# Decoder step on one core: the heads' inverse on 32x32 blocks, one sample part, unbroken scores, w_out in two halves of the tokens

## The chip, the core and the metric

The kernel runs on one core of a Trainium2 chip. The metric is the device time of one execution in microseconds (us). Five engines work side by side, each through its own list of instructions in a fixed order: TensorE (PE, matrix products into PSUM), VectorE (DVE), ScalarE (ACT), GpSimd (POOL) and SyncE (SP, which issues most of the DMA transfers).

## What is computed

The reference is one layer of a decoder trunk in fp32. 512 tokens of a prompt and 8 requests of 4 sample tokens share the weights; the kernel works on all 544 at once.

```python
def trunk_layer(x, wkv0, shift0, conv0, p):
    x = layer_norm(ALPHA * x + 0.5 * swiglu(x, ffn1), ln1)
    proj = x @ p["w_in"]
    # RWKV-7 heads: r, k, v, decay w, a, gate g from the token-shifted part of proj; per token
    #   sa = S (-kk);  S = S * w + sa (kk * a)^T + v k^T;  o = S r
    y_rwkv = group_norm(o) + sum(r * k * r_k) * v, times g
    # short conv: u = c_c * c_h; z = cw[0] u[t] + cw[1] u[t+1] + cw[2] u[t+2]
    y_conv = c_b * z
    mix = concat([y_rwkv, y_conv]) @ p["w_out"]
    x = layer_norm(ALPHA * x + mix, ln2)
    return layer_norm(ALPHA * x + 0.5 * swiglu(x, ffn2), ln3), states
```

There are 8 heads of size 64, a model width of 1024 and an FFN width of 2816. The outputs are the tokens and the new states of the heads, the shift and the convolution.

## The kernel before

**Large products.** Weights and activations are split into a high and a low fp32r part (`split`, `wsplit`: ACT writes the high part, DVE the low part, L146 and L147 for weights), and a 128x128 weight block is applied in three products (`mm3`). The trace calls their PSUM tiles `mm` (3 buffers) and the other ones `sm` (5 buffers). A weight tile of 1024 columns comes through a ring of raw buffers and a ring of split buffers `hl`; `ex_hl` lengthens the second ring for a while.

**Stages.** FFN1 and its norm; projections; the heads and the convolution (the mixer); w_out with the second norm; FFN2 and the last norm. FFN1 and FFN2 lie outside the change. Tokens go in two halves, of 256 and of 288 (`HALF`).

**The heads.** Four pairs of heads, eight chunks of 64 prompt tokens and a ninth one for the 32 sample tokens. For each pair `scores` makes the triangular products of its chunks (into `SC`), stores the strict triangle A to DRAM (`Ad`), and transposes k and v into `BK` and `UV`; `off` then masks A to what lies off its 16x16 diagonal blocks. `elim` inverts the 64 unit triangular 64x64 matrices: the 16x16 diagonal blocks are gathered from DRAM, one to a partition and half (`AT`), and inverted on DVE in 15 steps of two instructions (L982, L984; result `De`); `De` and its transpose are written into zero-filled 64x64 frames in DRAM (`Dd`, filled at L823 to L829 from a part of UV that POOL clears), read back as `DM` and `XT`, and four rounds of 64 products with 64, 48, 32 and 16 columns finish the inverse in `XT`. Each round's results leave PSUM through ACT or DVE; after the first, POOL copies UV into SC (L1020). `sample` treats the ninth chunk, in two parts of two pairs: inverse of 4x4 blocks (`X8`), products with the loaded state (`S0`), W, UV, outputs, and for each head pair a masked copy `ux` (L1165) and a 512-wide product that updates the state. `chain` then goes through the eight chunks in order, three dependent groups of small products a chunk (W, UV, S).

**What sets the order.** The program is written out as generators. Critical ones (`scores`, `elim`, norms) yield a price; `weave` spends that price, times a factor of `FILL`, on the background list `bg` of large products (the projections of the convolution, then w_out). `take(n)` spends an absolute amount. In `elim` the background is an alternation (`alt`) of `sample` and the convolution. A scheduler may move instructions of an engine among independent ones; while `pinned` is set, PE keeps the written order.

**w_out.** After the chain the four tiles of the convolution rows (`wo_c`) run for both halves, woven with the norm of the heads (`gnorm`, four calls); then the four tiles of the head rows (`wo_r`), kept in the ring of 3+4, run for half 0 alone and for half 1 behind the second norm of half 0 (`l2a`). That is 96 large products behind the norm. The split of FFN2's first weights follows on ACT.

## Time and profile before

| | |
|---|---|
| median of 3 runs | 1123.34 us (1118.27 to 1123.51) |
| profiled execution | 1127.86 us, of which span 1126.1 us |
| granted TensorE clock, mean | 0.986 |
| PE busy | 1093.6 us (97%) |
| DVE, ACT, POOL busy | 833.2, 573.5, 198.5 us |
| chain that ended last | PE 89%; DMA, DVE and ACT 3% each |
| first scores of the last pair, first product of `sample` | 535.8 us, 549.0 us |
| start of the chain, end of the chain | 626 us, 662 us |
| end of w_out, first product of FFN2 | 728 us, 733 us |

The span runs from the first to the last instruction of the profiled execution; its own time is 1.8 us longer. Busy time is the sum over an engine's instructions without overlaps. A row of the timeline has start, duration, engine, line of the program, operation, `out<-in`, shape and count. An fp32 product of the small kind is two instructions in the trace, so 64 products stand as x128.

### The profile page before, as it was taken

To read this page: it belongs to the slowest core of one execution; us is meant where nothing else is said; L and a number is where in the kernel's file an instruction comes from. 1 tells how busy PE (TensorE), PEld (TensorE's weight loads), DVE (VectorE), ACT (ScalarE), POOL (GpSimd) and SP (SyncE) were. 2 spreads that over 40 slices of the span, in tenths; PEclk is the share of its full clock that TensorE was granted. 3 is DMA by queue.
4 is the path that set the end of the run, shared out by engine and by line. 5 is a ranking of instruction groups with operands and counts; after the bars stand their busy time and mean duration, and the time that the engine had idled before them with its cause. 6 is when DMAs were issued, how large, how long until landed. Compare 5 with 4: busy or idle time off the path is not lost.

```text
span 1126.1 us, 23085 instructions
## 1 busy us (share of the span) xinstructions
PE 1093.6 (97%) x9432; PEld 1047.8 (93%) x9432; DVE 833.2 (74%) x1521; ACT 573.5 (51%) x1056; POOL 198.5 (18%) x319
## 2 busy tenths in 40 slices
PE   9999999999999999999998899899999999999996
PEld 8999999999999988999887689899999999999995
DVE  7788988888776857667653556778979888896655
ACT  6645556555552574554213554367455565554524
POOL 0131221303100133132101420001312213131000
PEclk9999999999999999999998899989999999999999
DMA  8576685958751372312473511143676949586402
GB/s 291 114 155 166 141 199 126 216 130 185 165 161 41 117 153 67 86 49 70 113 103 115 178 60 57 41 150 76 136 185 131 208 111 220 141 171 145 118 1 80
DMA packets 100523, 145.64 MB, mean 129 GB/s; under 512 B 38976, under 2 KB 62912, under 8 KB 100416
## 3 DMA queue, kind: packets, MB, share of 16 engines
q1 hardware_dynamic: 73216, 107.97, 31.8%
q0 software_dynamic: 27200, 36.18, 20.9%
q8 instruction: 74, 1.21, 0.4%
q14 instruction: 33, 0.27, 0.1%
HBM read 124.70 MB, written 10.52 MB: 120 GB/s over the span
## 4 chain that ended last, share of the span: by engine, by line
PE 89%; DMA 3%; DVE 3%; ACT 3%; issue 1%; SPq 1%; POOL 0%; ACTq 0%; DVEq 0%
PE mm L75 55%; PE sm L75 34%; DMA z<-sv 1%; DMA DM<-Dd 1%; ACT hl L146 1%; DMA raw<-in_wd 1%; DVE hl L147 0%; DMA z<-in_xT 0%; SPq L697 0%; DMA yc<-ycd 0%; DMA BK<-in_w 0%; DVE z L261 0%; ACT z L252 0%; ACT L135 0%; DVE xhl L269 0%
## 5 line engine op out<-in xcount | busy, mean ns | idle before, releaser
L75 PE MATMUL mm<-xhl,hl 128*128 128x256 f32 (+2 forms) x2640 | 372.7, 296 | 5.8 <-ACT hl L146 5.0
L75 PEld LDWEIGHTS mm<-xhl,hl 128*128 128x128 f32 x2640 | 347.0, 191 | 20.8 <-issue 7.1
L147 DVE TENSOR_TENSOR hl<-raw,hl 128x1024 fp32r<-128x1024 f32 (+3 forms) x224 | 260.7, 1169 | 65.7 <-ACT hl L146 64.9
L146 ACT ACTIVATE hl<-raw 128x1024 fp32r<-128x1024 f32 (+3 forms) x224 | 224.2, 1012 | 80.0 <-DVE raw L486 31.1
L75 PE MATMUL sm<-xhl,hl 128*128 128x272 f32 (+1 forms) x1392 | 193.7, 289 | 0.4 <-DVE xhl L151 0.3
L75 PEld LDWEIGHTS sm<-xhl,hl 128*128 128x128 f32 x1392 | 182.0, 189 | 1.6 <-DVE xhl L151 0.8
L75 PE MATMUL mm<-tv,hl 128*128 128x272 f32 x864 | 122.0, 290 | 2.4 <-ACT cpb L586 2.4
L75 PE MATMUL mm<-hhl,hl 128*128 128x272 f32 (+2 forms) x792 | 119.2, 294 | 0.1
L75 PEld LDWEIGHTS mm<-tv,hl 128*128 128x128 f32 x864 | 114.0, 189 | 3.0 <-ACT cpb L586 2.6
L75 PEld LDWEIGHTS mm<-hhl,hl 128*128 128x128 f32 x792 | 105.9, 188 | 5.1 <-ACT sv L625 1.5
L75 PE MATMUL sm<-hhl,hl 128*128 128x272 f32 (+2 forms) x792 | 109.5, 288 | 0.0
L75 PEld LDWEIGHTS sm<-hhl,hl 128*128 128x128 f32 x792 | 102.9, 188 | 0.5
L492 POOL DMA_DIRECT2D raw<-in_gu x36 | 43.5, 1209 | 259.0 <-DVE cpb L582 84.3
L498 POOL DMA_DIRECT2D raw<-in_wd x32 | 39.3, 1470 | 279.2 <-DVE hlb L151 245.7
L75 PE MATMUL mm<-tv,hlb 128*128 128x272 f32 x432 | 61.1, 291 | 0.9 <-ACT cpb L589 0.9
L75 PEld LDWEIGHTS mm<-tv,hlb 128*128 128x128 f32 x432 | 56.4, 188 | 2.5 <-ACT cpb L589 2.4
L217 ACT ACTIVATE lnq<-z 128x512 f32<-128x512 f32 (+1 forms) x24 | 15.0, 654 | 53.7 <-DVE z L216 53.7
L150 ACT ACTIVATE hhl<-sv 128x272 fp32r<-128x272 f32 (+1 forms) x52 | 26.0, 512 | 30.5 <-DVE sv L349 12.1
L151 DVE TENSOR_TENSOR hlb<-raw,hlb 128x512 fp32r<-128x512 f32 x52 | 35.7, 686 | 5.5 <-ACT hlb L150 5.5
L150 ACT ACTIVATE hhl<-hk 128x272 fp32r<-128x272 f32 (+1 forms) x48 | 24.2, 504 | 27.5 <-DVE hk L556 12.9
L486 DVE TENSOR_TENSOR raw<-raw 128x512 f32<-128x512 f32 x52 | 35.8, 688 | 1.0
L75 PE MATMUL mm<-hhl,hlb 128*128 128x272 f32 (+2 forms) x264 | 36.4, 288 | 0.0
(300 smaller groups left out, 1391.7 us busy)
## 6 DMA issues: line engine op xcount, KB each, us to landing
raw<-in_gu SPq DMA_DIRECT2D x84, 512.0 KB, 4.7
raw<-in_gu POOLq DMA_DIRECT2D x36, 512.0 KB, 6.5
raw<-in_wd SPq DMA_DIRECT2D x32, 512.0 KB, 4.8
raw<-in_win SPq DMA_DIRECT2D x26, 512.0 KB, 3.5
raw<-in_wd POOLq DMA_DIRECT2D x32, 256.0 KB, 6.4
raw<-in_wd SPq DMA_DIRECT2D x16, 384.0 KB, 3.1
z<-cpb POOLq DMA_DIRECT2D x16, 272.0 KB, 8.8
z<-sv POOLq DMA_DIRECT2D x16, 272.0 KB, 7.5
```

What stands on the lines that cost most here:

```text
L75: ins = f(*args, **kw)
L146: ACT.activation(hl[:, 0, a:b], raw[:, a:b], AF.Copy)
L147: DVE.tensor_tensor(hl[:, 1, a:b], raw[:, a:b], hl[:, 0, a:b].bitcast(F32), op=OP.subtract)
L150: ACT.activation(hi, x, AF.Copy)
L151: DVE.tensor_tensor(lo, x, hi.bitcast(F32), op=OP.subtract)
L217: sq = ACT.activation(qq, zz, AF.Square)
L486: DVE.tensor_tensor(y[:, :, 0], y[:, :, 1], a[:, :, 1], op=OP.add)
L492: POOL.dma_start(x.rearrange("p (s c) -> p s c", s=2), bass.AP(tensor=a11.tensor, offset=a11.offset, ap=[[2 * D, P], [P * 2 * D, 2], [1, 5 ...
L498: POOL.dma_start(four(x)[:, i], bass.AP(tensor=a11.tensor, offset=a11.offset, ap=[[DFF, P], [P * DFF, 2], [1, 256]]), accum_op=OP.add)
```

## The change

1. **Inverse.** Blocks of 32x32, 31 steps of two instructions on up to 256 elements per partition (L964, L966 of the changed program); the results go to DRAM as whole rows of 4 KB, come back in pieces of 128 B, only the diagonal blocks, with no zero-filled frame; two rounds of 64 products 32x32 take the place of four. `off`, its mask and the zero fill are gone; POOL clears XT.
2. **Sample.** One part for all four pairs. The state comes in one transfer of 1 MB. One of the two `ux` of a pair and the last scaling of the state move from DVE to POOL.
3. **Scores.** The stops inside a pair go but for one of 600; PE is pinned there; the fills ahead of pairs become 2500 in place of 2000.
4. **w_out.** All eight weight tiles stay (ring 3+5). Order: convolution rows of half 0 beside the head norm of half 0, head rows of half 0 beside the norm of half 1, then all rows of half 1 behind the second norm, 192 products. PE is unpinned after the chain.

```diff
-FILL = dict(..., p0=2000, s=0.4, p3=2000, e0=1.0, e1=1.0, g=1.5, l2a=1.0, ...)
+FILL = dict(..., p0=2500, s=600, p3=2500, e0=1.0, e1=1.0, g0=1.0, g1=1.0, l2a=1.5, ...)
...
-    POOL.memset(uvf[:, 0:2048], 0.0)
...
-    for d in Dd:
-        for par in range(2):
-            dma(d[par, :, 0:64].rearrange("c s t -> s c t"), uvf[R(par), 0:2048].rearrange("p (c t) -> p c t", t=64))
+    Dd = [dr.tile([2, 32, 2, 32, 32], F32, name=f"Dd{i}") for i in range(2)]
...
-                yield 400
...
-            if p < 3:
-                self.off()
...
-        for g in range(2):
-            dma(AT[:, g], diag(Ad, g))
+        dma(AT, bass.AP(tensor=Ad.tensor, offset=Ad.offset, ap=[[2080, P], [64, 32], [1, 32]]))
...
+        for k in range(31):
+            n = 31 - k
+            tv = tm[:, :n * (k + 1)].rearrange("p (i j) -> p i j", j=k + 1)
+            DVE.tensor_tensor(tv, AT[:, k, k + 1:32, None].to_broadcast([P, n, k + 1]),
+                              De[:, k, None, 0:k + 1].to_broadcast([P, n, k + 1]), op=OP.mult)
+            DVE.tensor_tensor(De[:, k + 1:32, 0:k + 1], De[:, k + 1:32, 0:k + 1], tv, op=OP.add)
+            yield 550
+        DVE.tensor_copy(AT, De.rearrange("p a b -> p b a"))
         for d, x in zip(Dd, (De, AT)):
+            dma(d.rearrange("a c b s t -> (a c b) s t"), x)
+        B = lambda par, b: slice(64 * par + 32 * b, 64 * par + 32 * b + 32)
+        for i, (x, b) in enumerate(((DM, 0), (XT, 1), (XT, 0))):
             for par in range(2):
+                dma(x[B(par, b)].rearrange("p c d t -> p (c d) t")[:, :, 32 * b:32 * b + 32],
+                    Dd[i > 0][par, :, b].rearrange("c s t -> s c t"))
...
-        for rnd in range(4):
+        for rnd in range(2):
+            for c0 in range(0, 8, 4):
                 q = sm()
+                for c in range(c0, c0 + 4):
                     for pl, par in PLP:
+                        o = ((c - c0) * 4 + pl) * 32
+                        a, b = B(par, rnd), B(par, 1 - rnd)
+                        if rnd:
+                            lhs, rhs = DM[a, c, pl, :], XT[a, c, pl, 32:64]
+                        else:
+                            lhs, rhs = SC[a, pl, par, c, 32:64], DM[a, c, pl, :]
+                        PE.matmul(q[b, o:o + 32], lhs, rhs, start=True, stop=True)
...
-    def sample(g, cp):
+    def sample(cp):
...
+                (POOL if par else DVE).tensor_tensor(ux[par], UV[:, pl, par, 8, None, :].to_broadcast([P, NSEQ, 64]),
+                                  bmask[:, :, None].to_broadcast([P, NSEQ, 64]), op=OP.mult)
...
+            POOL.tensor_tensor(s0v, s0v, Pes[:, pl, :, None].to_broadcast([P, NSEQ, 64]), op=OP.mult)
...
-        weave("s", pairs[p].scores())
+        pinned[0] = True
+        for _ in pairs[p].scores():
+            take(FILL["s"])
+        pinned[0] = False
...
-    wstate["ex_hl"] = [lambda: w4.tile([P, 2, 1024], F32R, name="hl", bufs=4)] * 4
+    wstate["ex_hl"] = [lambda: w4.tile([P, 2, 1024], F32R, name="hl", bufs=5)] * 5
...
+    wc = [wload(wo_c[i]) for i in range(4)]
+    wr = [wload(wo_r[i]) for i in range(4)]
+    bg.append(wout(wc, KC, 0))
+    weave("g0", seq(gnorm(0, 0, yp), gnorm(1, 0, yp)))
     drain()
+    bg.append(wout(wr, KR, 0, True))
+    weave("g1", seq(gnorm(0, 1, yp), gnorm(1, 1, yp)))
+    drain()
+    bg.append(seq(wout(wc, KC, 1), wout(wr, KR, 1, True)))
     weave("l2a", layer_norm(z, 0, V_LN2G, V_LN2B, epsl, lnq, lnr, f2.s1[0], to_x(z, False)))
```

Three places in the order of instructions. The first is PE at the rounds of the inverse, before: `DM,SC` is the first round, `XT,DM` are the later ones, `xhl,hl` the convolution's large products, and `X`, `AR,S`, `SI` belong to the second part of `sample`.

```order
L75 MATMUL mm<-xhl,hl 128x288 x10
L75 MATMUL mm<-xhl,hl 128x256 x24
L75 MATMUL sm<-DM,SC 64x64 x60
L75 MATMUL sm<-XT,DM 64x48 x32
L75 MATMUL mm<-xhl,hl 128x288 x21
L75 MATMUL sm<-AR_4711,S_6761 64x2x4 x16
L75 MATMUL sm<-XT,DM 64x48 x32
L75 MATMUL sm<-AR_4711,S_6761 64x2x4 x16
L75 MATMUL sm<-XT,DM 32x32 x64
L75 MATMUL sm<-SI,SC 64x64 x4
L75 MATMUL sm<-XT,DM 16x16 x32
```

After, the same place up to the first product of the chain's second step (`W,XT`):

```order
L75 MATMUL mm<-xhl,hl 128x288 x17
L75 MATMUL sm<-DM,SC 32x32 x2
L75 MATMUL mm<-xhl,hl 128x288 x7
L75 MATMUL mm<-xhl,hl 128x256 x19
L75 MATMUL sm<-DM,SC 32x32 x62
L75 MATMUL mm<-xhl,hl 128x256 x5
L75 MATMUL mm<-xhl,hl 128x288 x10
L75 MATMUL sm<-XT,DM 32x32 x2
L75 MATMUL mm<-xhl,hl 128x288 x14
L75 MATMUL sm<-UV,SC 64x64 x8
L75 MATMUL sm<-XT,DM 32x32 x62
L75 MATMUL sm<-W_7311,XT 64x64 x4
```

There are two rounds left, the sample's products are no longer among them (they all stand ahead), and 62 pieces of the second round stand between the chain's first product (`UV,SC`) and its second. From the first product of `sample` to the first `DM,SC` there are 337 large products now and 194 before; from the first scores to the start of the chain they are 906 in both programs.

The second is DVE at the end of the elimination steps, before: `tm` and `De` are a step, `cu` is the convolution's product, `ux` and `S` belong to `sample`, `hl` is a weight split.

```order
L1248 TENSOR_TENSOR cu<-zc,mm 128x256
L984 TENSOR_TENSOR De<-De,tm 128x2x2x14
L1170 TENSOR_TENSOR S_6493<-S_6493,sm 128x512
L982 TENSOR_TENSOR tm<-AT,De 128x30
L1120 TENSOR_TENSOR X_6766<-sm,cs 32x2x32
L984 TENSOR_TENSOR De<-De,tm 128x2x15
L1171 TENSOR_TENSOR S_6493<-S_6493,Pes 128x512
L986 COPY AT<-De 128x512
```

After, where `zc<-zc,mm` is the convolution's last product of a row of blocks:

```order
L1230 TENSOR_TENSOR zc<-zc,mm 128x256
L964 TENSOR_TENSOR tm<-AT,De 128x87
L966 TENSOR_TENSOR De<-De,tm 128x3x29
L964 TENSOR_TENSOR tm<-AT,De 128x60
L1230 TENSOR_TENSOR zc<-zc,mm 128x288
L966 TENSOR_TENSOR De<-De,tm 128x2x30
L964 TENSOR_TENSOR tm<-AT,De 128x31
L966 TENSOR_TENSOR De<-De,tm 128x31
L968 COPY AT<-De 128x1024
L147 TENSOR_TENSOR hl<-raw,hl 128x1024
```

The state's update is no longer among the last steps, and the result of a large product (`zc<-zc,mm`, half 1) stands ahead of the last three instructions and the copy.

The third is ACT at the end of w_out and the start of FFN2, before: L268 writes the normed tokens, L217 squares for the norm of half 1, and L146 splits FFN2's weights, of which `hl_8776` is the one that PE takes first.

```order
L268 ACTIVATE xhl_68<-z_7467,vc_66 128x256 x3
L146 ACTIVATE hl_8854<-raw_8853 128x1024
L268 ACTIVATE xhl_68<-z_7467,vc_66 128x256 x3
L146 ACTIVATE hl_8921<-raw_8920 128x1024
L268 ACTIVATE xhl_68<-z_7467,vc_66 128x256 x2
L146 ACTIVATE hl_8776<-raw_8775 128x1024
L146 ACTIVATE hl_8781<-raw_8780 128x1024
L217 ACTIVATE lnq_8771<-z_7467 128x576 x2
```

After, where PE takes `hl_8601` first:

```order
L268 ACTIVATE xhl_68<-z_7292,vc_66 128x256 x8
L146 ACTIVATE hl_8679<-raw_8678 128x1024
L146 ACTIVATE hl_8746<-raw_8745 128x1024
L217 ACTIVATE lnq_8596<-z_7292 128x576
L146 ACTIVATE hl_8601<-raw_8600 128x1024
L217 ACTIVATE lnq_8596<-z_7292 128x576
L146 ACTIVATE hl_8606<-raw_8605 128x1024
```

All eight writes of the norm now stand ahead of the splits, and one square stands between the second and the third split.

More of the change, by code (lines that the diff above doesn't have):

```diff
@@ L953, in scores @@
                 DVE.tensor_tensor(vf[:, t0:t1], vf[:, t0:t1], q[:, :t1 - t0], op=OP.mult)
-            if p < 3:
-                self.off()
-        def off(self):
-            for par in range(2):
-                sc = SC[R(par), self.p, par, 0:8, 0:64]
-                DVE.tensor_tensor(sc, sc, offm[R(par), None, :].to_broadcast([64, 8, 64]), op=OP.mult)
-    def diag(d, g):
-        return bass.AP(tensor=d.tensor, offset=d.offset + g * 1040 * P, ap=[[1040, P], [64, 16], [1, 16]])
     PLP = [(pl, par) for pl in range(4) for par in range(2)]
@@ new lines, in elim @@
+                        o = ((c - c0) * 4 + pl) * 32
[5 more added lines that the diff above has]
+                        PE.matmul(q[b, o:o + 32], lhs, rhs, start=True, stop=True)
+                for par in range(2):
+                    b = B(par, 1 - rnd)
+                    dst = XT[b, c0:c0 + 4, :, 32:64] if rnd else DM[b, c0:c0 + 4]
+                    src = q[b].rearrange("p (c d t) -> p c d t", c=4, d=4)
+                    (ACT.copy if par else DVE.tensor_copy)(dst, src)
@@ L1018, in elim @@
+                yield 0
             if rnd == 0:
@@ L1023, in v2, with v4 @@
         return q[rows, :128].rearrange("p (d t) -> p d t", d=2)
+    def v4(q, rows=slice(0, P)):
+        return q[rows, :256].rearrange("p (d t) -> p d t", d=4)
     def chain(XT, tl):
@@ L1140, in sample @@
         q = sm()
-        for pl in range(2):
-            for par in range(2):
-                PE.matmul(q[R(par), pl * 64:pl * 64 + 64], SC[:, 2 * g + pl, par, 8, 0:64], SI[:, pl, par, :], start=True,
-                          stop=True)
-        W = tl([P, 2, 64], F32, name="W")
-        ACT.activation(W, v2(q), AF.Copy)
-        yield 450
-        q = sm()
-        for pl in range(2):
-            for par in range(2):
-                PE.matmul(q[R(par), pl * 64:pl * 64 + 64], X8[R(par), pl, :], W[R(par), pl, :], start=True, stop=True)
@@ new lines, in sample @@
+        W = tl([P, 4, 64], F32, name="W")
+        ACT.activation(W, v4(q), AF.Copy)
+        yield 900
+        q = sm()
+        for pl, par in PLP:
+            PE.matmul(q[R(par), pl * 64:pl * 64 + 64], X8[R(par), pl, :], W[R(par), pl, :], start=True, stop=True)
+        DVE.tensor_copy(UV[R(0), :, 0, 8, :], v4(q, R(0)))
+        ACT.copy(UV[R(1), :, 1, 8, :], v4(q, R(1)))
+        yield 900
+        q = sm()
+        for pl, par in PLP:
+            PE.matmul(q[R(par), pl * 64:pl * 64 + 64], UV[:, pl, par, 8, :], SC[:, pl, par, 8, 64:128], start=True, stop=True)
@@ new lines, in sample @@
+        DVE.tensor_tensor(O[:, :, 8, 0:32], WT, v4(q)[:, :, 0:32], op=OP.add)
+        yield 900
+        for pl in range(4):
+            q = sm()
+            ux = []
+            for par in range(2):
+                ux.append(tl([P, NSEQ, 64], F32, name=f"ux{par}"))
+                (POOL if par else DVE).tensor_tensor(ux[par], UV[:, pl, par, 8, None, :].to_broadcast([P, NSEQ, 64]),
+                                  bmask[:, :, None].to_broadcast([P, NSEQ, 64]), op=OP.mult)
+            yield 900
+            for par in range(2):
+                PE.matmul(q[R(par), :], BK[:, pl, par, 8, :], ux[par].rearrange("p b i -> p (b i)"), start=True, stop=True)
@@ L1301, in body @@
     est = ExitStack()
-    DM = pool(est, "dm").tile([P, 8, 4, 64], F32, name="DM")
+    DM = pool(est, "dm").tile([P, 8, 4, 32], F32, name="DM")
     el = elim(XT, DM)
-    bg.appendleft(alt(seq(sample(0, cp), sample(1, cp)), bg.popleft() if bg else iter(())))
-    weave("e0", islice(el, 17))
+    bg.appendleft(alt(sample(cp), bg.popleft() if bg else iter(())))
+    weave("e0", islice(el, 32))
     weave("e1", el)
```

148 lines of the change are left out of this document (44 added, 104 removed).

## The prediction

> **What bounds the kernel now.** I read the table of stretches first, to see where TensorE is not full. Columns: stretch, its length, busy time (and instructions) of PE, PEld, DVE, ACT and POOL, the granted TensorE clock, the DMA share, GB/s.
>
> ```profile
> 300.00:325.00 25.00, 25.00 (x201) 25.00 (x200) 18.90 (x27) 13.96 (x24) 1.32 (x2) 1.00 0.52 132
> ...
> 575.00:600.00 25.00, 23.91 (x339) 23.03 (x339) 7.39 (x16) 5.57 (x10) 4.83 (x11) 1.00 1.07 189
> 600.00:625.00 25.00, 22.34 (x467) 17.04 (x467) 13.23 (x29) 6.46 (x16) 1.45 (x3) 0.86 0.10 34
> 625.00:650.00 25.00, 20.23 (x378) 17.27 (x376) 12.38 (x33) 15.46 (x43) 14.46 (x40) 0.86 0.56 199
> ...
> 725.00:750.00 25.00, 20.68 (x121) 18.36 (x120) 19.62 (x34) 15.49 (x26) 0.00 (x0) 0.86 0.50 168
> ```
>
> In the first row, one of an FFN, PE is busy for all of its 25 us: there only fewer products would help. It falls short between 575 and 750 us, in the elimination, the chain and the start of FFN2, and three of these stretches ran at a granted clock of 0.86. Second, the list of what PE waited for (total us, times, longest):
>
> ```profile
> PE mm L75 <- ACT hl L146: 5.0, 3, 3.9
> PE sm L75 <- issue: 3.0, 3, 2.4
> PE sm L75 <- DMA DM<-Dd: 0.8, 1, 0.8
> ```
>
> The longest entry is 5.0 us of 1126. So the time is PE's own, and a product, a break or a wait that leaves PE's line between the scores and FFN2 leaves the total nearly one for one. Third, the PE groups of the elimination's rounds (busy us, mean ns, idle before them), of which each fp32 product is two instructions:
>
> ```profile
> L75 PE MATMUL sm<-DM,SC 64*64 64x64 f32 x128 | 4.8, 221 | 0.8 <-DMA DM<-Dd 0.8
> L75 PE MATMUL sm<-XT,DM 64*64 64x48 f32 x128 | 4.4, 218 | 0.3 <-issue 0.3
> L75 PE MATMUL sm<-XT,DM 64*32 64x32 f32 x128 | 2.5, 193 | 0.3 <-issue 0.3
> L75 PE MATMUL sm<-XT,DM 64*16 64x16 f32 x128 | 2.2, 179 | 2.4 <-issue 2.4
> ```
>
> Fourth, the PE timeline from the first sample product (548.99) to the chain's second step (627.91); a bracket is the idle time before a row:
>
> ```profile
> 548.99 0.22 PE L75 MATMUL sm<-cs,SC 32*32 32x32 f32 x2
> ...
> 583.74 1.09 PE L75 MATMUL mm<-xhl,hl 128*128 128x288 f32 x7
> 585.58 0.44 PE L75 MATMUL sm<-DM,SC 64*64 64x64 f32 x4 [0.75 <-DMA DM<-Dd]
> ...
> 611.69 1.03 PE L75 MATMUL sm<-XT,DM 64*16 64x16 f32 x63 [2.41 <-issue]
> 612.66 0.69 PE L75 MATMUL sm<-SC,UV 128*64 128x64 f32 x8
> ...
> 614.98 1.94 PE L75 MATMUL mm<-xhl,hl 128*128 128x288 f32 x7
> 616.85 1.26 PE L75 MATMUL sm<-ux,BK 128*64 128x512 f32 x2
> ...
> 627.91 0.68 PE L75 MATMUL sm<-W,XT 64*64 64x64 f32 x16 [1.06 <-ACT W L1052]
> ```
>
> **The change, part by part.** The sum is made against the profiled execution, 1127.86 us (span 1126.1), which lies 4.5 us above the median of 1123.34; differences are carried over unchanged.
>
> *Inverse, on PE: -10.7.* The four rounds hold 4.8+4.4+2.5+2.2 = 13.9 us of busy time and 0.3+0.3+2.4 = 3.0 of idle time, 16.9 in all, less about 1.0 by which groups overlap their neighbours: 15.9. Two rounds of 128 small pieces remain. Their nearest row is 64x32 at 2.5 us; with 0.1 of idle each that is 5.2. If the after-rounds also wait 0.5 each for their evictions, it is -9.7.
>
> *The half clock: -1.9.* Behind the 2.41 us hole, 7 of the large products took 1.94 instead of 1.09 us (the rows at 614.98 and 583.74). From 612.66 to 616.85 are 4.2 us, and at 1.09/1.94 of that 1.85 go away if no such hole is left. The profile's clock bears it: 0.86 in 600 to 625. A wait of 0.75 us had no such effect (1.00 in 575 to 600). The Trainium skill ("TensorE: Matmul & The Clock Gate", Part 1) has the gate close after an idle window of about 3.4 us; by that rule a hole of 2.4 us need not be the cause, the term would be nothing, and the sum 1.9 smaller. The row decides here, and the low value stays in the range.
>
> *Read-back of the diagonal: +0.25 (-0.75 to +3).* The 0.75 us wait may vanish or grow, since the steps on DVE grow from 30 instructions to 62.
>
> The DVE groups of that part (count, busy us, mean ns):
>
> ```profile
> L147 DVE TENSOR_TENSOR hl<-raw,hl 128x1024 fp32r<-128x1024 f32 x8 | 9.7, 1218 | 1.8 <-ACT hl L146 1.8
> ...
> L982 DVE TENSOR_TENSOR tm<-AT,De 128x30 f32<-128x30 f32 x2 | 0.4, 188 | 0.6 <-DMA AT<-Ad 0.6
> ...
> L984 DVE TENSOR_TENSOR De<-De,tm 128x128 f32<-128x128 f32 x1 | 0.3, 285 | 0.0
> ```
>
> 30 elements cost 188 ns, 128 cost 285: 0.99 ns an element on a base of 158. The 62 new steps have 10,912 elements: 62 x 0.158 + 10.8 = 20.6, and 0.03 between dependents makes 22.5 us. Among them stand four weight splits (4.9) and smaller rows, by order and such prices some 17 us in all: DVE has 40 us of work. PE takes 248 large products (30.8 us at 0.124) and nearly all of the sample's small ones (about 19 with their breaks, an estimate) up to the convolution result that stands in front of DVE's last three steps, of which about 5 pass before AT is there: some 45 us. So DVE is not late by load, but the last steps wait for that result. Behind it PE has 89 large products until it asks for DM, 11 us at 0.124 each. Against that: the last steps (1.0), De to DRAM, DM back.
>
> The transfers (count, KB, us from issue to landing):
>
> ```profile
> S<-in_s SPq DMA_DIRECT2D x2, 512.0 KB, 4.5
> ...
> DM<-Dd SPq DMA_DIRECT2D x2, 512.0 KB, 9.0
> ```
>
> De is now 512 KB in 4 KB rows; the nearest row is the state load, 4.5 us. DM's read has half as many packets as before, 2048; half of its 9.0 is 4.5, and 3.5 to 5 is my estimate. Together 9 to 10.5 against 11: no wait if all goes well, up to 3 us if DVE slips by 2 and the read competes with the other 512 KB write. I take 1.0 of wait, less 0.75.
>
> *Breaks in PE's line: -1.4.* Each change from large products to small ones and back costs something. In the norm of the heads:
>
> ```profile
> 674.44 1.06 PE L75 MATMUL mm<-xhl,hl 128*128 128x256 f32 x6
> 675.34 0.59 PE L75 MATMUL sm<-O,cs 128*128 128x256 f32 x2
> ...
> 698.93 13.18 PE L75 MATMUL mm<-xhl,hl 128*128 128x288 f32 x108
> ```
>
> 108 large products end 13.0 us after their start, 0.12 each; six of them before a break take 0.90 instead of 0.72. That is 0.2 a break, and in the written order there are 40 instead of 47 between the first scores and the chain. The large products there are the same 906. Nothing if the breaks only move.
>
> *Chain start: -1.5 (0.5 to 2.6).* The 1.06 us wait for W at 627.91 gets 62 pieces of the second round in front of it, which cover it. Of the further waits in the first two steps I count 0.4.
>
> *Scores unbroken: +1.0 (0 to 3).* Off-diagonal masks (8 DVE instructions) go, off PE's path. In return up to eight PSUM results are made in a row, with 89 fewer large products woven in from the first scores on.
>
> ```profile
> L922 DVE TENSOR_TENSOR SC<-sm,cs 128x512 f32<-128x512 f32 x4 | 2.6, 684 | 2.3 <-PE sm L75 2.3
> ```
>
> ```profile
> 547.44 0.46 PE L75 MATMUL sm<-cs,bkb 64*128 64x64 f32 x7 [0.21 <-ACT BK L948]
> ```
>
> An eviction takes up to 0.68 us, and PE has waited 0.21 for one already where no large products stood between; with five buffers I count one such wait for each pair.
>
> *One sample part: +0.5 (0 to 2).* Half the serial steps, counted under breaks. The state now comes as one transfer behind the read of AT instead of half of it ahead; at 4.5 us per 512 KB it lands 5 to 9 us after the part begins, and PE wants it after about 10. The second ux and the scaling move to POOL, eight instructions; they lie beside 89 more large products than before.
>
> *w_out in halves: +1.5 in the first norm (0 to 2.5).* The stretch of the first norm and of its 96 large products, columns as in the first table:
>
> ```profile
> 661.90:682.80 20.90, 19.45 (x123) 17.98 (x121) 15.45 (x31) 12.88 (x24) 0.00 (x0) 0.92 0.41 133
> ```
>
> The three more weights that are split beside the first norm cost DVE 3 x 1.22 = 3.7 us; DVE had 5.4 us idle in the 20.9 us, part of it unavoidable at its start. The rest is the same 384 products.
>
> *FFN2's start: -1.7 (+0 to -3.5).*
>
> ```profile
> 727.58 0.74 PE L75 MATMUL sm<-cpb,ones 128*128 128x288 f32 x2
> 728.33 0.75 PE L75 MATMUL sm<-z,ones 128*128 128x288 f32 x2
> 732.99 0.54 PE L75 MATMUL mm<-xhl,hl 128*128 128x256 f32 x2 [3.91 <-ACT hl L146]
> ...
> 735.22 3.17 PE L75 MATMUL mm<-xhl,hl 128*128 128x256 f32 x12
> ```
>
> ```profile
> 729.99 1.04 ACT L146 ACTIVATE hl<-raw 128x1024 fp32r<-128x1024 f32 x1
> ...
> 733.79 1.24 ACT L217 ACTIVATE lnq<-z 128x576 f32<-128x576 f32 x2
> ```
>
> ```profile
> 731.36 0.74 DVE L216 TENSOR_TENSOR z<-z,sm 128x576 f32<-128x576 f32 x1
> ```
>
> FFN2's first product came 5.4 us after the end of w_out, and the steady run 7.6 us after it, since two splits into w_out's old buffers and five of the norm's writes stood ahead of its own split on ACT. With 96 more products behind the norm, those writes are done early. What is left is one split (1.04), one square (0.62, startable 2.3 us after w_out's end: 1.5 for the mean, 0.74 for the subtraction) and the wanted split (1.04): about 4.0, and the steady run at 5.8, since DVE does four subtractions ahead of its half of the split. The idle time doesn't vanish: a split into a buffer of w_out still waits for its last product, with the wanted one queued behind it.
>
> Sum: -10.7 -1.9 +0.25 -1.4 -1.5 +1.0 +0.5 +1.5 -1.7 = -13.9. By the profiled execution 1114.0, by the median **1109.4**.
>
> **The rivals.**
> *The elimination on DVE becomes the bound (slower).* PE then stands before DM for as long as the chain of 62 dependent steps is late. It eats the whole gain at 14 us of lateness beyond a slack of about 1; slower by 5.6 needs 20, which is 0.33 us on each step, nearly double its 0.36. Time at that point 1129, and 1135 with the steps at 0.8. For it: the new form of the operands (two broadcasts) has no row at over 128 elements. Against: the line through 30 and 128 is straight. Chance 0.08.
>
> *POOL's eight new instructions hold DVE up (half the gain).* They read 128x512 from SBUF beside the steps, which read two operands. The rows of a POOL copy at one shape:
>
> ```profile
> L896 POOL COPY UV<-at 64x512 f32<-64x512 f32 x8 | 7.5, 941 | 0.2
> ...
> L1020 POOL COPY SC<-UV 64x512 f32<-64x512 f32 x8 | 4.9, 610 | 16.8 <-PE sm L75 16.4
> ```
>
> Beside DVE work POOL needs 0.94 instead of 0.61: POOL waits. If DVE waited in its place, eight times about 1 us less the slack gives back 6.5: 1116. The Trainium skill ("SBUF — State Buffer", Who interferes with whom) says that a DVE instruction with two SBUF inputs and a GpSimd instruction that reads SBUF lock each other out, whoever issued first; the trace shows one side of that. Chance 0.13.
>
> *No change.* The read-back slips by 4 us, a half clock follows as it did behind 2.41 us (2 to 3.4), and scores and norm cost their upper ends (+2 and +1): 10 given back, about 1120. For it: convolution rows that wait for PE stand between DVE's steps, so one late row delays all. Chance 0.14.
>
> *More than forecast.* FFN2's start fills entirely (3.7 beyond the term above) and a half clock of 1.9 goes with it: 1104, with other good ends 1100. Against: the order on ACT. Chance 0.10.
>
> That the change doesn't do what it says can be excluded for the rounds (their products are gone), not for the scores, in whose gaps the order still shows a few large products; that is worth 1 us.
>
> **How the numbers follow.** The forecast (1104 to 1115) has 0.55. No difference under 0.5%, 5.6 us, can be told from no change here. Faster by more, below 1117.7: 0.55 + 0.10 + most of POOL's case, 0.11 = 0.76. Within: 0.14 + 0.02 = 0.16. Slower: 0.08. The range: the terms at their good ends, -10.7 -1.9 -0.75 -1.4 -2.6 -3.5, give -20.9, 1102.5, and the case above reaches 1100: I take 1101; at their bad ends, -9.7 +2.25 -0.5 +3 +2 +2.5 and nothing else, -0.5. I cut that at 1120, the no-change case, which leaves out the slower rival and the tails.
>
> **What would show it.** In the profile after: two groups of 128 small pieces of 2.5 to 2.7 us; 575 to 650 with a clock of 1.00 until the chain; a wait for DM under 2 us; from the first sample product to the chain's first W 74 to 79 us (78.9 before) with 89 more large products in it; 5 us from the end of w_out to FFN2. Wrong would be: a wait for DM over 4 us, steps of 256 elements over 0.45 us, POOL's or the state's name ahead of PE, or a norm stretch over 23 us.

## The result, and the profile after

The changed kernel takes 1105.26 us (median of 4 runs, 1103.74 to 1107.86), the kernel before 1123.42 beside it (4 runs, 1118.27 to 1124.61): a ratio of 0.9849 [0.9811, 0.9888], 18.2 us by the medians. Forecast were 13.9 us and 1109.4. The profiled execution took 1107.86, its span is 1106.1, 20.0 less than the span before. Three executions of kernels measured further below, one with the sample part alone and two with two sample parts, took 1736 to 3343 us, and the ratios leave them out.

To see where, I cut both traces at the same six landmarks: first scores, first product of `sample`, first `W,XT` of the chain, first `O,cs` of the head norm, end of w_out (first `cpb,ones`), and the end of the 24th large product of FFN2. Columns as in the table of stretches. Before:

```profile
430.39:548.99 118.60, 117.96 (x1106) 109.28 (x1105) 83.70 (x143) 56.36 (x123) 30.59 (x74) 1.00 0.27 75
548.99:627.91 78.92, 74.10 (x1088) 61.95 (x1088) 41.22 (x104) 18.16 (x42) 8.48 (x22) 0.96 0.51 104
627.91:661.93 34.02, 29.68 (x608) 25.37 (x608) 15.57 (x49) 18.96 (x60) 20.50 (x56) 0.90 0.37 130
661.93:727.57 65.64, 64.11 (x447) 60.67 (x445) 43.53 (x95) 24.71 (x49) 0.00 (x0) 0.97 0.20 67
727.57:739.89 12.32, 8.00 (x32) 6.48 (x31) 12.32 (x21) 10.24 (x16) 0.00 (x0) 0.73 0.32 100
```

After:

```profile
432.29:538.27 105.98, 105.07 (x1017) 97.65 (x1016) 72.75 (x125) 53.37 (x118) 22.59 (x67) 1.00 0.24 69
538.27:614.13 75.86, 75.28 (x921) 65.53 (x921) 49.29 (x117) 14.48 (x29) 21.57 (x40) 0.98 0.41 114
614.13:645.50 31.37, 28.34 (x611) 23.76 (x608) 15.39 (x49) 19.16 (x61) 18.63 (x48) 1.00 0.32 109
645.50:709.56 64.06, 62.91 (x447) 59.67 (x445) 50.06 (x108) 31.11 (x58) 0.00 (x0) 1.00 0.29 93
709.56:719.34 9.78, 7.95 (x38) 6.08 (x37) 8.88 (x10) 7.59 (x9) 0.00 (x0) 0.83 0.49 147
```

Scores and elimination belong together, since 89 large products moved from the first stretch to the second: -12.62 and -3.06, -15.7. The chain gives -2.65, w_out -1.6, the start of FFN2 -2.5. That is -22.4; outside these stretches 2.4 came back, 1.9 of them ahead of the first scores (430.4 us before, 432.3 after). Over all the traces below the first scores lie between 430.4 and 435.8 us, so this is spread and no price of the change. Two quantities go with the gain. PE's idle time (length less PE's busy time, summed) falls from 15.7 to 7.5 us. And the clock: a stretch of T us at a granted clock of c lacks T x (1 - c) of full-speed time. Before that is 3.2 + 3.4 + 2.0 + 3.3 = 11.9 us, after 1.5 + 0 + 0 + 1.7 = 3.2. How much of the 8.7 is time depends on whether PE's rate sets the pace there.

The table of 25 us stretches after, against the one shown of before:

```profile
550.00:575.00 25.00, 24.42 (x225) 17.22 (x221) 16.92 (x38) 4.23 (x8) 10.04 (x11) 0.93 0.07 22
...
600.00:625.00 25.00, 23.75 (x529) 21.08 (x528) 9.88 (x26) 11.09 (x30) 10.71 (x26) 1.00 0.47 139
625.00:650.00 25.00, 22.76 (x440) 19.28 (x441) 13.74 (x39) 15.34 (x45) 13.11 (x32) 1.00 0.14 37
```

From 600 us to the end of the chain the clock is at 1.00 now. A shortfall is left at the start of FFN2 (0.83 in the last stretch above), and there is a new one behind 550.

What PE waited for:

```profile
PE sm L75 <- ACT lnq L217: 3.2, 2, 1.8
...
PE sm L75 <- ACT BK L942: 0.9, 4, 0.2
...
PE mm L75 <- ACT hl L146: 0.5, 2, 0.3
```

The 5.0 us for `hl` are 0.5, and `DM` is not in the list any more. Part of the wait for `hl` has moved to the norm's squares: `lnq` has 3.2 us, 1.4 before. The groups of the rounds and the transfers around them:

```profile
L75 PE MATMUL sm<-XT,DM 32*32 32x32 f32 x128 | 2.5, 192 | 0.0
L75 PE MATMUL sm<-DM,SC 32*32 32x32 f32 x128 | 2.5, 192 | 0.0
```

```profile
Dd<-De SPq DMA_DIRECT2D x1, 512.0 KB, 2.8
...
DM<-Dd SPq DMA_DIRECT2D x2, 128.0 KB, 4.5
```

And PE's timeline from the last large products of the elimination to the chain:

```profile
575.37 25.94 PE L75 MATMUL mm<-xhl,hl 128*128 128x288 f32 x204
601.23 0.31 PE L75 MATMUL sm<-DM,SC 32*32 32x32 f32 x4
...
604.85 2.21 PE L75 MATMUL sm<-DM,SC 32*32 32x32 f32 x124
...
611.99 2.21 PE L75 MATMUL sm<-XT,DM 32*32 32x32 f32 x124
```

None of these rows has a bracket: PE waits for nothing between 575 and 615. `DM` lands about 4.5 us after its issue at 595, so 1 to 2 us before PE asks for it.

### The profile page after: what moved, and what is told of

Same layout as the page of the kernel before. It is cut to its first block, busy times and chain, and to the rows that moved or that the text cites. A ratio compares the mean times of both kernels' runs of the same rounds, so it can differ in the third digit from the quotient of the medians.

```text
span 1106.1 us, 22515 instructions
## 1 busy us (share of the span) xinstructions
PE 1078.5 (98%) x9176; PEld 1035.7 (94%) x9176; DVE 833.0 (75%) x1520; ACT 570.7 (52%) x1042; POOL 201.9 (18%) x320
## 4 chain that ended last, share of the span: by engine, by line
PE 78%; DMA 7%; DVE 6%; ACT 4%; issue 4%; SPq 0%; POOL 0%; ACTq 0%; DVEq 0%; POOLq 0%
PE mm L75 50%; PE sm L75 29%; DMA z<-cpb 2%; DMA raw<-in_gu 2%; DVE hl L147 2%; ACT hl L146 2%; DMA z<-sv 1%; DMA raw<-in_wo_r 1%; DVE hhl L151 1%; DMA raw<-in_wd 1%; DMA z<-in_xT 1%; DVE z L609 0%; SPq L697 0%; DMA BK<-in_w 0%; ACT z L252 0%
## 5 line engine op out<-in xcount | busy, mean ns | idle before, releaser
L75 PE MATMUL mm<-xhl,hl 128*128 128x288 f32 (+2 forms) x2640 | 367.9, 294 | 0.9 <-ACT xhl L150 0.5
L146 ACT ACTIVATE hl<-raw 128x1024 fp32r<-128x1024 f32 (+3 forms) x224 | 224.6, 1012 | 92.0 <-DVE raw L486 31.3
L492 POOL DMA_DIRECT2D raw<-in_gu x36 | 43.5, 1209 | 258.4 <-DVE cpb L582 83.4
L217 ACT ACTIVATE lnq<-z 128x512 f32<-128x512 f32 (+1 forms) x24 | 15.1, 654 | 42.9 <-DVE z L216 42.9
```

What stands on the lines that cost most here:

```text
L75: ins = f(*args, **kw)
L146: ACT.activation(hl[:, 0, a:b], raw[:, a:b], AF.Copy)
L217: sq = ACT.activation(qq, zz, AF.Square)
L492: POOL.dma_start(x.rearrange("p (s c) -> p s c", s=2), bass.AP(tensor=a11.tensor, offset=a11.offset, ap=[[2 * D, P], [P * 2 * D, 2], [1, 5 ...
```

## The experiments

Two questions stood behind them. Are the parts' gains terms of a sum, as the prediction had them, or does one part only pay with the others in place? And did the hole ahead of the last rounds lower the clock, or something else? Ratios are to the kernel before, run on the same chip, with a 95% interval; the stretches are those of above, from each kernel's trace, in us ("S+E": scores and elimination together). Each stretch comes from one execution. Two traces of the changed kernel differ by 1.5 us in S+E, and kernels with the same start of FFN2 by 1.4 us there, so a difference of 1 to 1.5 us in these columns says nothing.

| kernel | median | ratio | S+E | chain | w_out | FFN2 |
|---|---|---|---|---|---|---|
| before, profile | | | 197.5 | 34.0 | 65.6 | 12.3 |
| after | 1105.26 | 0.9849 [0.9811, 0.9888] | 181.8 | 31.4 | 64.1 | 9.8 |
| after, again | 1106.61 | 0.9834 [0.9812, 0.9856] | 183.3 | 31.4 | 64.4 | 9.8 |
| inverse alone | 1127.05 | 1.0015 [0.9991, 1.0039] | 200.3 | 32.1 | 65.6 | 10.8 |
| sample part alone | 1121.03 | 0.9958 [0.9941, 0.9976] | 191.6 | 33.4 | 64.4 | 11.0 |
| inverse + sample part | 1117.77 | 0.9935 [0.9915, 0.9955] | 189.2 | 32.4 | 64.4 | 12.2 |
| after, old inverse | 1114.64 | 0.9901 [0.9886, 0.9917] | 192.5 | 30.0 | 64.0 | 9.8 |
| after, two sample parts | 1117.37 | 0.9932 [0.9908, 0.9956] | 193.1 | 33.1 | 63.9 | 8.4 |
| the same, tiles released later | 1111.36 | 0.9863 [0.9842, 0.9883] | 185.9 | 30.7 | 64.4 | 10.0 |
| after, old scores | 1110.57 | 0.9863 [0.9820, 0.9906] | 184.2 | 31.9 | 64.4 | 9.8 |
| after, old w_out | 1113.93 | 0.9887 [0.9830, 0.9944] | 183.3 | 33.9 | 64.2 | 12.2 |
| after, `ux` on DVE | 1113.60 | 0.9893 [0.9875, 0.9912] | 187.9 | 31.3 | 63.9 | 8.4 |
| after, state products spread | 1106.77 | 0.9829 [0.9809, 0.9849] | 182.4 | 31.4 | 64.8 | 9.8 |
| after, FFN2 first | 1105.89 | 0.9819 [0.9798, 0.9840] | 181.8 | 32.4 | 64.7 | 5.7 |

Taken back one at a time and set against the change repeated, the four parts are worth 0.67% (inverse), 0.98% (sample), 0.29% (scores, not clear of noise) and 0.53% (w_out). That is 2.5% in all, where the whole change is worth 1.7%. The parts are not terms of a sum.

**The inverse alone, in the kernel before.** The edit is part 1 of the change and nothing else:

```diff
-        for k in range(15):
+        for k in range(31):
...
-        for rnd in range(4):
+        for rnd in range(2):
...
     bg.appendleft(alt(seq(sample(0, cp), sample(1, cp)), bg.popleft() if bg else iter(())))
-    weave("e0", islice(el, 17))
+    weave("e0", islice(el, 32))
```

> The kernel before with the new inverse alone (32x32 blocks, two rounds, no zero-filled frame, no masks); sample, scores and w_out as before. Theory A (most of the gain is the inverse: 11 us of products, and the half clock behind them goes too): 11 to 14 us faster than before, rounds of 2.5 us each, no clock below 1.00 between 600 and 627 us. Theory B (the gain is the sum of many small repairs in the order; the inverse gives its products but loses some to the longer steps): 5 to 8 us faster, with a wait for DM of 3 us or more in front of the first round.

It gained nothing, 1.0015 [0.9991, 1.0039], and so missed both expectations. PE's waits, and the clock where they fall:

```profile
PE sm L75 <- DMA DM<-Dd: 5.3, 2, 4.9
...
PE sm L75 <- ACT W L1032: 4.1, 1, 4.1
```

```profile
600.00:625.00 25.00, 18.91 (x235) 16.64 (x233) 14.46 (x35) 5.95 (x9) 2.65 (x6) 0.81 0.54 130
625.00:650.00 25.00, 19.67 (x368) 14.80 (x366) 10.90 (x24) 13.35 (x34) 13.44 (x32) 0.71 0.51 187
```

The last step ends at 611.1, behind the second sample part's DVE work, and `DM` is back at 618.5: PE stands 4.9 us for it. Later PE stands 4.1 us for W. The clock lacks 25 x (0.19 + 0.29) = 12.0 us over these two rows, where before it lacked 25 x 0.28 = 7.0. Some of it falls into the waits, where it costs nothing. The 10 us of products that were saved are spent on the two waits and on the clock around them. This is the rival with the elimination as the bound, though not by slower steps (255 elements took 0.41 us here).

**The sample part alone, and with the inverse.** The edits are part 2 in the kernel before, then parts 1 and 2:

```diff
-    bg.appendleft(alt(seq(sample(0, cp), sample(1, cp)), bg.popleft() if bg else iter(())))
+    bg.appendleft(alt(sample(cp), bg.popleft() if bg else iter(())))
```

> The kernel before with the single sample part alone (its copies and scalings on POOL); inverse, scores and w_out as before. Theory C (inverse and sample part pay off together): the part ends before the rounds do, the wait for W at the chain's start goes, the half clock at 600 to 625 us may go with it; 3 to 7 us faster than before. Theory D (the sample part carries most of the gain by itself): 10 us or more faster.

> The kernel before with both the new inverse and the single sample part, scores and w_out as before. If the two were additive it would be what the sample part alone gives (the inverse alone gave 0). Theory C: the read-back is in time (no wait for DM over 1 us), W doesn't wait, and the total is 12 to 15 us faster than before, at least 6 us below the better of the two alone. Theory D: not more than 2 us below the sample part alone.

The single part alone gives 0.42% [0.24, 0.59], the two together 0.65% [0.45, 0.85]. The first, some 5 us, is what was expected if the two parts need each other (3 to 7). The second misses: 12 to 15 us were expected of the pair and some 7 came. The intervals overlap, so it is not shown that the inverse adds anything here. From PE's waits from 535 to 735 of the kernel with both:

```profile
PE sm L75 <- DMA DM<-Dd: 1.7, 1, 1.7
```

The wait for W is gone and that for `DM` has shrunk from 4.9 to 1.7. The 89 large products that unbroken scores leave to the elimination are not what is still missing. The changed kernel with old scores (below) doesn't have them there either; its trace shows no wait for `DM`, S+E is 184.2 where it is 189.2 here, and its ratio is 0.9863. It differs from this kernel by the w_out part alone, so that part counts together with the others; by which step was not looked into.

**The old inverse in the changed kernel.** The edit of the first experiment, backwards (15 steps, four rounds, `off`, frames).

> The changed kernel with the inverse as before (16x16 blocks, four rounds, zero-filled frame, masks), everything else as changed. Theory C (the inverse and the single sample part need each other: alone, the inverse gave 0): the sample part ends early here too, so the wait for W at the chain's start is under 1 us; the four rounds cost their 11 us again; total 9 to 12 us above the changed kernel, 1114 to 1117. Theory D (the gain is the sample part and the order; the inverse adds little): within 3 us of the changed kernel.

0.9901 [0.9886, 0.9917] against 0.9834 for the change repeated: the inverse is worth some 0.67% here, 7.5 us. In scores and elimination it is 192.5 against 183.3 and 181.8 in the two traces of the change, 9.1 to 10.6, near the size forecast. With everything else in place PE no longer waits for the 62 steps, and only then does most of the term arrive.

**Two sample parts in the changed kernel**, all their work on DVE as before:

```diff
-    def sample(cp):
+    def sample(g, cp):
...
-        S0 = tl([P, 4, NSEQ, 64], F32, name="S0")
+        S0 = tl([P, 2, NSEQ, 64], F32, name="S0")
...
-    bg.appendleft(alt(sample(cp), bg.popleft() if bg else iter(())))
+    bg.appendleft(alt(seq(sample(0, cp), sample(1, cp)), bg.popleft() if bg else iter(())))
```

> The changed kernel with the sample in two parts of two pairs, its copies and scalings all on DVE. Breaks 46 instead of 40: 1.2 us more. The tiny state products (64x8) no longer stand in one run of 128, so that the half clock at 553 us should go if they cause it (1.7 us less), and stay if it has another cause. DVE's steps of 256 elements all near 0.41 us instead of up to 1.14. Total within 1.5 us of the changed kernel; 3 us or more longer would say that the serial steps of the second part count.

This costs the most of the four parts, about 1%, where less than 1.5 us were expected; some of it can be POOL's share, which went back to DVE with it (0.6% by itself, below). PE at the start of the chain, and what ACT waited for from 600 to 640:

```profile
626.98 1.12 PE L75 MATMUL sm<-W,XT 64*64 64x64 f32 x16 [4.42 <-ACT W L1033]
```

```profile
ACT W L1033 <- DMA out_wkvs<-S: 2.8, 1, 2.8
```

ACT, which writes the chain's W, waits for the store of the sample's state, issued at 621.9. No data of the one goes into the other; but the sample's tiles are released ahead of the chain (`sst_.close()`), and the chain's tiles take their place. If so, releasing them later must take the wait away:

```diff
     est.close()
-    sst_.close()
     prs.close()
...
     cst0.close()
+    sst_.close()
```

> The changed kernel with the sample in two parts as before, but its tiles are kept until after the chain, so that the chain's W and S lie elsewhere and need not wait for the store of the sample's state. If that store is what PE waits 4.4 us for at the chain's first W, that wait falls under 1 us, the half clock behind it goes and the total falls by 4 to 7 us against the run with two parts, to within 3 us of the changed kernel. If W waits for something else, nothing changes.

PE's row at that place in this kernel:

```profile
618.47 0.68 PE L75 MATMUL sm<-W,XT 64*64 64x64 f32 x16 [1.30 <-ACT W L1033]
```

The wait falls from 4.4 to 1.3, and the ratio from 0.9932 [0.9908, 0.9956] to 0.9863 [0.9842, 0.9883]. Scores and elimination fall from 193.1 to 185.9, but some 3 us of that are a low clock at 545 us in the first of the two traces, 75 us ahead of the wait (shown further down), and the second trace is the fastest of its four executions: the ratio is the firmer number. So most of what two parts cost is a reused tile, and one thing that a single part brings is that its store leaves early. After the change it is issued at

```profile
578.57 0.34 SPq L1150 DMA_DIRECT2D out_wkvs<-S  x1
```

36 us ahead of the chain. The store is what W waits for in the inverse alone too (2.4 us of ACT's time there), and already in the kernel before, whose list of ACT's waits from 600 to 640 has

```profile
ACT W L1052 <- DMA out_wkvs<-S: 1.8, 1, 1.8
```

That a later release takes the wait away was tried only with two sample parts in the changed kernel.

**POOL's share taken back to DVE** (`ux` and the scaling of the state):

```diff
-                (POOL if par else DVE).tensor_tensor(ux[par], ...
+                DVE.tensor_tensor(ux[par], ...
...
-            POOL.tensor_tensor(s0v, s0v, Pes[:, pl, :, None].to_broadcast([P, NSEQ, 64]), op=OP.mult)
+            DVE.tensor_tensor(s0v, s0v, Pes[:, pl, :, None].to_broadcast([P, NSEQ, 64]), op=OP.mult)
```

> The changed kernel with the eight instructions that went to POOL (four masked copies, four scalings, 128x512) back on DVE. If POOL's reads hold DVE's two-input steps up, the steps of 240 to 256 elements that took 0.76 to 1.14 us beside POOL are all at 0.40 to 0.42; DVE gets 5.5 us more work of its own instead of the 2.3 us it lost. The total changes by less than 1.5 us either way, as the read-back has some 2 us to spare; over 3 us more would say that DVE's load is what bounds the elimination.

In the changed kernel some steps are long. DVE's timeline there, then POOL's groups from 538 to 632:

```profile
565.01 0.42 DVE L966 TENSOR_TENSOR De<-De,tm 128x252 f32<-128x252 f32 x1
567.12 0.76 DVE L964 TENSOR_TENSOR tm<-AT,De 128x255 f32<-128x255 f32 x1
...
577.67 1.14 DVE L964 TENSOR_TENSOR tm<-AT,De 128x247 f32<-128x247 f32 x1
```

```profile
L1148 POOL TENSOR_TENSOR S<-S,Pes 128x512 f32<-128x512 f32 x4 | 4.8, 1206 | 4.1 <-DVE S L1147 4.1
L1141 POOL TENSOR_TENSOR ux<-UV,cs 128x512 f32<-128x512 f32 x4 | 4.8, 1192 | 6.0 <-ACT UV L1129 4.8 <-PE sm L75 1.1
```

With POOL's eight instructions gone every step is back at its price. DVE's group of 255 elements in this kernel, and PE's waits from 535 to 660:

```profile
L964 DVE TENSOR_TENSOR tm<-AT,De 128x255 f32<-128x255 f32 x2 | 0.8, 412 | 0.0
```

```profile
PE mm L75 <- DVE zc L1230: 2.4, 1, 2.4
PE sm L75 <- DVE ux L1141: 1.5, 1, 1.5
```

So POOL does hold DVE up: the long steps lose some 2.5 us in all. But without POOL DVE has the eight instructions itself (0.68 us each in this trace, 5.5 us), PE waits 2.4 and 1.5 us for it, and the kernel is slower by about 0.6% than the change, 6.6 us where less than 1.5 were expected. Some 3 us more of DVE's time are already too much: DVE's load sits close to the bound of the elimination. The split between the engines pays although they hinder each other. The Trainium skill ("SBUF — State Buffer", Who interferes with whom) says that a DVE instruction with two SBUF inputs and a GpSimd instruction that reads SBUF contend, and that the order of issue decides who waits; with 0.41 us against 0.76 to 1.14 this case agrees that they contend, and shows DVE's side, which the trace of before did not. Who waits changes here too: POOL's first `ux` took 1.64 us beside a step at its usual 0.38; the order of issue was not put to a test.

**The old scores, and the old w_out.**

```diff
-FILL = dict(..., p0=2500, s=600, p3=2500, ...)
+FILL = dict(..., p0=2000, s=0.4, p3=2000, ...)
...
+                yield 400
...
-        pinned[0] = True
-        for _ in pairs[p].scores():
-            take(FILL["s"])
-        pinned[0] = False
+        weave("s", pairs[p].scores())
```

> The changed kernel with the scores broken up as before (stops inside a pair, not pinned, 603 large products ahead of the elimination instead of 514). By the count of breaks (42 instead of 40 from the first scores to the chain) 0.4 us more, and 0.7 us of waits for evictions less: within 1 us of the changed kernel. If unbroken scores are worth something of their own, first scores to start of the chain takes 2 us or more longer.

```diff
-    wstate["ex_hl"] = [lambda: w4.tile([P, 2, 1024], F32R, name="hl", bufs=5)] * 5
+    wstate["ex_hl"] = [lambda: w4.tile([P, 2, 1024], F32R, name="hl", bufs=4)] * 4
...
+    bg.append(wout(wo_c, (4, 5, 6, 7), (0, 1)))
+    weave("g", seq(*(gnorm(g, h, yp) for h in range(2) for g in range(2))))
```

> The changed kernel with the order of w_out as before (ring 3+4, 96 products behind the norm). Theory A: the part from the end of the chain to FFN2's steady run takes 2.6 us longer than in the changed kernel (1.6 in the head norm, 1.0 at FFN2's start, since five writes of the norm stand in front of the split again) and the total 2 to 3.5 us more, about 1108. Theory B: 4 us or more, since the half clock at FFN2's start doubles too. Rival: no difference, the stretch was shorter by chance.

With old scores S+E is 0.9 to 2.3 us longer than in the two traces of the change, hardly more than these differ from each other, and in the total the interval [0.9820, 0.9906] does not tell it from the change. What unbroken scores are worth is open. Old w_out brings the wait for `hl` at FFN2 back (3.90 us in one piece). That is 2.4 us at FFN2 and, unexpected, 2.5 in the chain, which w_out's order reaches only through its weight tiles. ACT's UV is late there (1.6), and the clock is below 1; why was not settled. The total, 0.53% or some 6 us with a wide interval, is more than the 2 to 3.5 us expected. The w_out stretch itself is 64.2, as with the new order.

**The state products spread.** After the change, the clock is low at 553, where there is neither a hole nor a wait. The PE row that precedes it, and the clock in steps of 5 us:

```profile
548.45 3.90 PE L75 MATMUL sm<-AR,S 64*64 64x8 f32 x128
```

```profile
550.00:555.00 5.00, 5.00 (x95) 4.73 (x92) 2.90 (x8) 2.05 (x4) 0.53 (x2) 0.80 0.00 0
555.00:560.00 5.00, 5.00 (x54) 4.08 (x53) 2.81 (x7) 1.12 (x4) 1.15 (x1) 0.86 0.37 110
```

PE is busy for all of the ten us. It is the single sample part that makes these 64 products with 8 columns into one run. I broke them up into eight groups with large products between:

```diff
+        pinned[0] = True
+        for _ in range(7):
+            yield 0
...
-        yield 3400
+                if b % 4 == 3:
+                    yield 425
+        pinned[0] = False
```

> The changed kernel, with the 128 tiny state products (64x8) in eight groups of 16 with six large products between them, instead of one run of 3.9 us; they stand a little later, and PE is pinned there. If a run of tiny products without any hole is what halves the clock at 553 us, the clock stays at 1.00 from 540 to 600 us. Seven more breaks cost about 1.4 us, the clock gives back about 1.7: total within 1 us of the changed kernel. If the half clock stays somewhere in 545 to 565, tiny products are not the cause.

The same place, then a stretch in which PE waited, and the first row behind that wait:

```profile
555.00:560.00 5.00, 5.00 (x82) 4.39 (x80) 4.34 (x12) 0.00 (x0) 0.24 (x2) 1.00 0.34 107
575.00:580.00 5.00, 2.39 (x19) 2.00 (x19) 4.97 (x7) 1.36 (x2) 2.95 (x3) 1.00 0.00 0
```

```profile
579.59 1.08 PE L75 MATMUL sm<-ux,BK 128*64 128x512 f32 x4 [2.61 <-DVE ux L1146]
```

In this trace the low clock is gone with the run. And a hole of 2.61 us, longer than the 2.41 that the prediction blamed, leaves the clock at 1.00, in this stretch and in the next (580 to 585). The time doesn't move (0.9829 against 0.9834): PE's waits for `ux` grow from 0.6 to 4.0 us, which can eat what the clock gave.

But one trace doesn't prove that the run is the cause, and the kernel with two sample parts speaks against so simple a rule. It was expected to have no low clock there if the run causes it, since its first products come as two groups of 32 instructions with six large products between. Below are its clock from 545 to 550 us, then the same stretch with the tiles released later, where PE's rows are the same and stand 1.3 us earlier:

```profile
545.00:550.00 5.00, 5.00 (x52) 4.73 (x51) 1.26 (x5) 0.43 (x2) 0.00 (x0) 0.50 0.33 105
```

```profile
545.00:550.00 5.00, 5.00 (x70) 4.53 (x67) 2.84 (x12) 0.97 (x4) 1.32 (x5) 1.00 0.35 108
```

The same products were followed by a clock of 0.50 in the one and 1.00 in the other. Over all the traces, the clock falls within or right behind the run of 128 in all nine that have it and behind the first two groups of 32 in two of four (in the inverse alone too, not in the kernel before). It does not fall behind the later runs of 64 in three traces, nor behind groups of 16 in the one trace. So the run of 128 goes with a fall, but the order of the products alone does not settle where one comes.

A hole beside small products is another matter than a hole alone. In the kernel with inverse and sample part, PE waits for `DM` and then runs the first round; the clock there:

```profile
614.12 3.04 PE L75 MATMUL sm<-DM,SC 32*32 32x32 f32 x125 [1.71 <-DMA DM<-Dd]
```

```profile
613.80:617.20 3.40, 2.98 (x130) 2.85 (x130) 1.07 (x3) 0.58 (x1) 0.23 (x1) 0.79 1.21 167
617.20:620.60 3.40, 2.62 (x68) 2.32 (x66) 0.68 (x1) 1.13 (x3) 3.11 (x6) 0.50 1.04 334
```

After the change the same round without a hole ran at 1.00 (the row of 600 to 625 above).

**FFN2's weights first.** What is left of the wait at FFN2 is queued on ACT. So its wanted split and DVE's half of it go ahead of the norm's first subtraction and square, and of a split that waits for w_out's last product:

```diff
+            if len(head) == 6:
+                after(i, head[2][0])
...
+            if j == 0 and table == "late" and len(head) > 2:
+                after(su, head[2][1])
+                after(sq, head[2][0])
```

> The changed kernel, with FFN2's first two weight splits on ACT and DVE ahead of the split that waits for w_out's last product and ahead of the norm's first subtraction and square. If the order behind that one split is what keeps FFN2 idle for 4.3 us, its first product comes within 1.5 us of the end of w_out and the run of products is steady by 3 to 4 us instead of 6.7: total 2 to 4 us below the changed kernel. If the buffer itself is needed to w_out's end, less than 1 us.

> The changed kernel itself once more, on the same chip as the three others, as their measure: 0.985 of the kernel before; the same landmarks within 1 us, and the half clock at 553 us again if it follows from the order of the products and not from chance.

PE in this kernel:

```profile
712.68 0.65 PE L75 MATMUL sm<-cpb,ones 128*128 128x288 f32 x2
...
713.77 0.61 PE L75 MATMUL mm<-xhl,hl 128*128 128x256 f32 x2
715.67 3.58 PE L75 MATMUL mm<-xhl,hl 128*128 128x256 f32 x28 [1.28 <-DVE hl L149]
```

FFN2's first product comes 1.1 us after the end of w_out, the 24th after 5.7 instead of 9.8. The total, 0.9819 [0.9798, 0.9840], is the lowest ratio measured, but not told apart from the change beside it (0.9834 [0.9812, 0.9856]): of the 4.1 us at the start of FFN2, 1.0 stands against it in the chain and the rest is within the spread. It beats the kernel before; that it beats the change is not shown.

## Why the prediction was right, and where its steps failed

The direction and the range held; 18.2 us were measured for 13.9. That the total came so close is in part luck: the largest term turned out to need the other parts, several terms were off, and they were off both ways. By stretches the terms compare so: scores and elimination -13.3 forecast (rounds, half clock, read-back, breaks, the wait for W, scores, sample part), -15.7 measured; chain -0.4 and -2.65; w_out +1.5 and -1.6; FFN2 -1.7 and -2.5. Beyond them are +2.4 that no term had, spread for the most part.

- **Rounds: right.** Two groups of 2.5 us; from 15.9 to about 4.8. The old inverse put back gives 9.1 to 10.6 in the stretch and 7.5 in the total. But the forecast took it as a term that stands by itself. It doesn't: in the kernel before it is worth nothing. The same change halves the sample's serial steps on DVE, lets its store leave early and has a new w_out, and with these the two waits are gone; how much each of them does was not separated, and the 89 more large products are not needed for it. The prediction had the sample part in view, but priced it at +0.5 and never asked what the inverse would be without it.
- **Half clock: right at its place, but neither the cause nor the sum.** From 600 us to the chain the clock is at 1.00 now, as forecast. That the 2.41 us hole was the cause is not shown: a hole of 2.61 us between large products leaves the clock at 1.00, and runs of small products without any hole are followed by a low one. The hole of before stood between small products, and beside such products 1.71 us went with a fall, so it can have had a share. And the clock lacked 11.9 us between first scores and FFN2, of which the sum counted 1.9, for the one place whose hole I had seen. After, 3.2 are missing. The surplus over the forecast is 8.5 us up to FFN2, and 6.8 more of clock came back than was counted; how much of that is time, and how much only stands beside a shorter wait, was not separated.
- **Read-back: mis-sized on the safe side.** The 0.75 us wait went and none came; write and read take 2.8 and 4.5 us, 7.3 together where 9 to 10.5 were estimated, and DVE's steps came at the forecast price (255 elements in 0.41 us).
- **Chain start: right in the result.** The wait for W is gone. Two things can cover it, the 62 pieces in front of W and the store that leaves 36 us ahead; with two sample parts the 62 pieces are there as well, and PE still waits 4.4 us. That the wait hangs on the sample's store was not seen; it is what could have made this term +4.
- **Scores: not confirmed.** The feared waits for evictions are there (0.9 in all, four times), but the +1.0 does not show: scores and elimination are 0.9 to 2.3 us shorter with unbroken scores than with the old ones, by single traces. The total does not tell the two apart.
- **Sample part: wrong sign.** Forecast as +0.5; undone, with POOL's share, it costs about 1%. POOL's lock, the rival at 0.13, is real (steps of 256 elements at 0.77 and 0.93, over the 0.45 named as a sign of error), but the 2.5 us were covered: `DM` is still back 1 to 2 us before PE asks for it.
- **w_out: the +1.5 did not come.** It stood for three more splits on DVE; DVE is busy 50.1 of 64.1 us there (43.5 of 65.6 before) and PE doesn't wait: its idle time is 1.15 us (1.53 before). The rest of the 1.6 goes with the clock, 0.97 to 1.00. Undoing w_out does not move this stretch (64.2), and the sample part alone has 64.4 with the old order, so it is not w_out's order that gave the 1.6. What the order is worth showed elsewhere, at FFN2 and in the chain.
- **FFN2: right.** First product at 4.3 us after w_out (4.0 forecast), with a wait for the square just ahead of it:

```profile
712.79 1.71 PE L75 MATMUL sm<-lnq,ones 128*128 128x288 f32 x4 [1.76 <-ACT lnq L217]
713.88 1.04 PE L75 MATMUL mm<-xhl,hl 128*128 128x256 f32 x2
...
716.23 6.01 PE L75 MATMUL mm<-xhl,hl 128*128 128x256 f32 x45
```

The steady run starts after 6.7 us where 5.8 were forecast.

## What to carry to other kernels

A saving on the bounding engine arrives only while everything that runs beside it still ends sooner: ask of each term what it would be if the other parts of the change were left out, and name the part that covers it. When two stages share a pool of tiles, a store at the end of the first is a wait at the start of the second, though no data passes. Sum the missing clock over all stretches before pricing one of them, and don't give it a cause on one coincidence: set all traces side by side that have the same products there.

## What the runs showed of the hardware

- **The clock fell while PE was busy without a gap.** 128 instructions of 64x8 in 3.9 us went with granted clocks of 0.80 and 0.86 in the two stretches of 5 us from 550, and in the change repeated with 0.69 and 0.63 there. With groups of 16 between large products it stayed at 1.00 in one trace; with groups of 32 it fell to 0.50 in one kernel and stayed at 1.00 in another with the same order. The Trainium skill ("TensorE: Matmul & The Clock Gate", Part 1) has the clock drop after an idle window of about 3.4 us: that 2.61 us of waiting did no harm agrees with it. A fall with PE never idle does not follow from that, and here the measurement decides. But small products alone don't always do it: in the kernel with the old inverse, PE's rounds of 64x64 to 64x32 and waits up to 1.28 us pass at full clock (1.00 from 575 to 600, with PE busy 20.7 of 25 us). The exact trigger is open, and so is the low clock of before between 600 and 675.
- **POOL and DVE:** beside a POOL multiply of 128x512 (1.2 us) a DVE step of 0.41 us took 0.76 to 1.14.
- **A store holds the tile that it reads.** The next stage's first write into the place of the sample's tiles waited for the store of the state (2.8 us of ACT's time, 4.4 of PE's), and with the tiles released later PE's wait was 1.3 us.
